# A hybrid encoder block on one core: branch A's order written out for four engines, gate traffic on ScalarE

## The chip, the cores and the metric

The kernel runs on one core of one Trainium2 chip. The metric is device time in microseconds. Five engines work side by side, each through its own stream of instructions in the order in which the program was built: TensorE (PE) multiplies matrices, VectorE (DVE) and POOL (GpSimd) work element by element, ScalarE (ACT) evaluates functions and copies, SyncE (SP) issues transfers. An instruction that waits holds up everything behind it in its stream. Transfers between SBUF (on the chip) and DRAM are carried out by 16 DMA engines after an engine has issued them; here "a store" goes to DRAM and "a load" comes from it.

## The reference

One layer of a block of 1024 positions, width 1024, with 16 meta positions ahead of them (1040 rows in all). All inputs and outputs are float32.

```
h = concat(meta, x)
proj = rms_norm(h) @ w_in            # qa, ka, va | qb, kb, vb | gate a, gate b
y_a  = differential_attention(...)   # 4 heads: softmax(q1 k1) - lam * softmax(q2 k2), times v,
                                     # bias -slope*|distance|, then rms_norm
y_b  = windowed_gqa(...)             # 8 heads, window 128, sinks
h = h + (sigmoid(ga) * (y_a @ w_ba) + sigmoid(gb) * (y_b @ w_bb)) @ w_o
h = h + (silu(f @ w_gate) * (f @ w_up)) @ w_down      # f = rms_norm(h), 2816 columns
out = rms_norm(h)[16:]
```

## The kernel before, in words

Products of float32 matrices are made of parts: an operand is split into a high part (ACT copies it to a rounded type) and a low part (POOL or DVE subtracts the high part from the operand), and three products are added: high*high, high*low, low*high. `split` at lines 117 and 118 makes both parts. Large products also use sums of blocks, so that seven products p = 1 to 7 of half the size stand for eight; the products of the two gates are done in this way, and their results are put together in DRAM: the results of p = 2, 3, 4 and 5 are copied out of PSUM by ACT (line 759) and stored (line 760); those of p = 1, 6 and 7 are added by DVE (line 756) to a kept value, which is loaded first (line 636) and stored again at line 760. A p = 3 step goes on in the PSUM bank of its p = 5 after that result was copied; p = 6, 7 and 4 go on in the bank of p = 1 in the same way. There are two such banks. Gate weights are loaded at line 624 (`gr`) and split into `gop`.

The stage that the change is about is branch A, the differential attention: 4 heads of 8 tiles of 128 queries. Per tile, map 1 and then map 0 each have three score products (line 814, 392 + 392 + 256 keys); DVE adds the distance bias and takes the minimum (line 817, accumulators `amn`), ACT takes the exponential with its sum (line 824, sums `adn`), DVE the reciprocal (line 826); POOL scales map 1 by the reciprocal and lambda (line 828), DVE joins the maps (line 837) and copies 32 columns (line 838). The joined weights of the tile before are then transposed on PE in three groups (line 849), ACT copies each out of PSUM as high part (line 852), DVE makes the low part (line 853). Every second tile the values are multiplied (line 862), every fourth one is normed (lines 869 to 885). Queries and keys of a head (`aq`, `ak`; lines 664 to 677) are loaded for map 1 and map 0 apart, as soon as the buffers are free in the last tile of the head before.

Gate products fill PE between the steps of a tile. What stands at each step is written in a string, `SLOTS = "sgsgsngsgsstntnt"`: s one score product, g one gate step (a quarter of a gate result: three products), t one group of transposes, n one part of values or norms. At the start of head 1, 2 and 3 ten gate steps come one behind the other (`G_HEAD = 10`) while the head's queries and keys arrive.

PE's order is written by hand ("manual schedule"): instructions go into PE's stream in the order of the code. For the other engines the framework's scheduler chose the order in branch A, but for the very first tile, where ACT and DVE were by hand too. At the start of the FFN (lines 1253 to 1400), DVE's order was by hand for the first twelve steps and ACT's was not. There the blocks of the normed rows are transposed, summed in pairs (`kept`, `ts`, `b`, lines 1268 to 1274) and split (line 1321, low parts 1325), and the weights are split at lines 117 and 118.

Transfers signal their end through eight semaphores, called DMAHW0 to DMAHW7 in the listings below, which all transfers of the program take in turn. A transfer whose turn has a semaphore in use waits for the transfer that uses it. Before, SP issued all of them.

## Time and profile before

| | us |
|---|---|
| median of 3 runs (lowest to highest) | 1441.89 (1441.3 to 1443.64) |
| profiled execution | 1441.88 |
| its span (first to last instruction) | 1440.0 |
| PE busy in it | 1420.1 |
| stage: norm, projections, branch B | 0 to 325 |
| stage: branch A with the gates | 325 to 615 |
| stage: sums of branches, output product | 615 to 812 |
| stage: FFN, gate and up | 812 to 1255 |
| stage: FFN, down, and final norm | 1255 to 1440 |

The ends of the stages are read from the timeline and rounded. PE is granted its full clock nearly throughout (0.998 as a mean).

How to read the rows: a row of the timeline is start, duration, engine and line, operation, what it writes and reads, shape, count; in brackets the idle time of the engine ahead of it, and what ended it. "SPq" is SP's issuing of transfers. A row of windows gives, for a stretch, its length, the busy time and number of instructions of PE, PE's weight loads, DVE, ACT and POOL, PE's granted clock, the busy share of the DMA engines and GB/s. A row of waits gives who waited, for what, the total, the number of times and the longest.

### The profile page before, as it was taken

The page shows a single profiled execution, that of the slowest core. Times are in us where ns is not written, and L with a number is a line of the kernel's source. Part 1 is how long each engine was busy: PE and PEld are TensorE (multiplying, and loading weights), DVE is VectorE, ACT ScalarE, POOL GpSimd, SP SyncE. Part 2 cuts the span into 40 slices and gives each one's busy share as a digit, 9 for nine tenths or more (in the row PEclk, how much of TensorE's full clock was granted, in tenths as well). Part 3 has the DMA queues.
Part 4 walks back from the last instruction along what each step waited for, and adds up shares of the span by engine and source line. Part 5 has one row for each costly group of instructions (what it writes and reads, how often), then busy time and mean ns, then how long its engine had stood idle before and what let it go on. Part 6 is the DMA issues. An engine that isn't in the chain of part 4 may idle for free.

```text
span 1440.0 us, 21175 instructions
## 1 busy us (share of the span) xinstructions
PE 1420.1 (99%) x7279; PEld 1219.3 (85%) x7279; DVE 899.8 (62%) x1624; ACT 680.1 (47%) x1294; POOL 643.6 (45%) x605
## 2 busy tenths in 40 slices
PE   8999999999999999999999999999999999999997
PEld 6988989988888989888888888888888888888886
DVE  7468536637787978624614886555555554787567
ACT  6366535545565656544413743333333333444444
POOL 5599127744433333334622665554454442000444
PEclk9999999999999999999999999999999999999999
DMA  8367668986657464576612535333323333964443
GB/s 246 87 211 235 194 160 275 282 284 221 181 178 257 145 224 141 175 251 207 210 49 88 162 93 176 99 106 105 110 97 101 104 103 102 340 201 142 124 129 139
DMA packets 188891, 242.41 MB, mean 168 GB/s; under 512 B 18208, under 2 KB 115936, under 8 KB 188784
## 3 DMA queue, kind: packets, MB, share of 16 engines
q1 hardware_dynamic: 188784, 241.07, 53.0%
q8 instruction: 57, 0.93, 0.3%
q14 instruction: 50, 0.41, 0.1%
HBM read 157.45 MB, written 77.00 MB: 163 GB/s over the span
## 4 chain that ended last, share of the span: by engine, by line
PE 86%; issue 3%; DMA 3%; POOL 3%; DVE 2%; ACT 2%; SPq 0%; POOLq 0%; ACTq 0%; DVEq 0%
PE pg L1347 28%; PE pd L1462 9%; PE pg L751 7%; PE ppa L796 6%; PE po L1105 6%; PE aps L814 4%; PE pp_ka L214 3%; PE pp_va L214 3%; PE pp_qa L214 3%; PE pp_qb L214 3%; PE apy L862 3%; POOL oa L118 3%; PE apt L849 2%; PE bpt L356 2%; PE bpy L362 2%
## 5 line engine op out<-in xcount | busy, mean ns | idle before, releaser
L118 POOL TENSOR_TENSOR wop<-wf,wop 128x512 fp32r<-128x512 f32 x128 | 172.0, 1348 | 165.5 <-ACT wop L117 153.1
L1347 PE MATMUL pg<-t,wop 128*128 128x512 f32 x1056 | 242.6, 389 | 0.0
L1347 PEld LDWEIGHTS pg<-t,wop 128*128 128x128 f32 x1056 | 198.3, 188 | 41.1
L1462 PE MATMUL pd<-ob,oa 128*128 128x512 f32 x924 | 210.0, 390 | 0.4 <-POOL oa L118 0.4
L1462 PEld LDWEIGHTS pd<-ob,oa 128*128 128x128 f32 x924 | 173.4, 188 | 36.9 <-POOL oa L118 0.8
L1347 PE MATMUL pg<-b,wop 128*128 128x512 f32 x792 | 183.5, 390 | 1.4 <-DVE kept L1272 1.4
L1347 PEld LDWEIGHTS pg<-b,wop 128*128 128x128 f32 x792 | 148.5, 188 | 32.3 <-issue 1.6
L751 PE MATMUL pg<-hT_hi,gop 128*128 128x512 f32 x384 | 142.4, 395 | 0.0
L117 ACT ACTIVATE wop<-wf 128x512 fp32r<-128x512 f32 x128 | 80.3, 632 | 86.9 <-PE pg L1347 47.7
L118 POOL TENSOR_TENSOR oa<-ra,oa 128x512 fp32r<-128x512 f32 x33 | 44.0, 1335 | 170.2 <-ACT oa L117 168.8
L118 POOL TENSOR_TENSOR gop<-gr,gop 128x512 fp32r<-128x512 f32 x47 | 65.5, 1395 | 102.8 <-ACT gop L117 101.7
L117 ACT ACTIVATE oa<-ra 128x512 fp32r<-128x512 f32 x77 | 48.7, 632 | 107.1 <-PE pd L1462 45.8
L824 ACT ACTIVATE as<-as,amn 128x1040 f32<-128x1040 f32 x64 | 74.5, 1164 | 48.6 <-DVE amn L817 37.7
L814 PE MATMUL aps<-ak,aq 128*128 128x392 f32 (+1 forms) x384 | 89.5, 328 | 2.7 <-DVE amn L817 2.1
L1163 DVE TENSOR_TENSOR s<-wf,wf 128x512 f32<-128x512 f32 x22 | 27.3, 1242 | 101.4 <-DMA wf<-in_w_ff_gate_dram 53.2
L1105 PE MATMUL po<-woh,mT 128*128 128x512 f32 x384 | 88.0, 390 | 0.0
L1105 PEld LDWEIGHTS po<-woh,mT 128*128 128x128 f32 x384 | 71.9, 188 | 14.8
L814 PEld LDWEIGHTS aps<-ak,aq 128*128 128x128 f32 x384 | 69.3, 188 | 16.2 <-DVE amn L817 3.3
L751 PEld LDWEIGHTS pg<-hT_hi,gop 128*128 128x128 f32 x384 | 72.3, 188 | 11.2 <-DVE gk L756 0.2
L343 POOL TENSOR_SCALAR bs<-bs,bdn 128x432 f32<-128x432 f32 (+1 forms) x64 | 41.4, 665 | 87.2 <-DVE bdn L341 74.5
L751 PE MATMUL pg<-hT_lo,gop 128*128 128x512 f32 x192 | 75.9, 395 | 0.0
L828 POOL TENSOR_SCALAR as<-as,adn,neglam 128x1040 f32<-128x1040 f32 x32 | 38.9, 1214 | 62.0 <-DVE adn L826 42.6
(292 smaller groups left out, 3101.7 us busy)
## 6 DMA issues: line engine op xcount, KB each, us to landing
ra<-aop SPq DMA_DIRECT2D x77, 256.0 KB, 2.6
wf<-in_w_ff_gate_dram SPq DMA_DIRECT2D x24, 512.0 KB, 3.8
wf<-in_w_ff_up_dram SPq DMA_DIRECT2D x24, 512.0 KB, 3.8
aop<-as SPq DMA_DIRECT2D x44, 256.0 KB, 2.1
w_c<-in_w_in_dram SPq DMA_DIRECT2D x17, 512.0 KB, 6.1
aop<-c SPq DMA_DIRECT2D x33, 256.0 KB, 2.0
ts_d<-to SPq DMA_DIRECT2D x16, 512.0 KB, 3.7
gw<-in_w_in_dram SPq DMA_DIRECT2D x32, 256.0 KB, 4.3
```

Source lines behind the costliest of these rows:

```text
L117: nc.scalar.activation(hi, src, AF.Copy)
L118: lo_eng.tensor_tensor(lo, src, f32(hi), ALU.subtract)
L214: nc.tensor.matmul(ps[:, :n], a[:, c, :], b[:, c, at:at + n], start=(c == 0 and i == 0), stop=(c == DC - 1 and i == 2))
L343: nc.gpsimd.tensor_scalar(st[:, r, :W], st[:, r, :W], dn[:, r:r + 1], 1.0, ALU.mult, ALU.mult)
L751: nc.tensor.matmul(ps, op[:, a, c], quad(b, *act)[:, c], start=(p in (2, 5, 1) and c == 0 and i == 0), stop=(p in (2, 3, 4) and c == 3 and ...
L796: nc.tensor.matmul(ps, w[:, a, j, :], src(j, b, tk), start=(j == 0 and n == 0), stop=(j == 3 and n == 2))
L814: nc.tensor.matmul(ps[:, :n], qs[m][:, t * P:(t + 1) * P], ks[m][:, vv, k0:k0 + n], start=(vv == 0), stop=(vv == 1))
L824: nc.scalar.activation(s[m][:, 0:L], s[m][:, 0:L], AF.Exp, bias=low, scale=-1.0, accum_out=dn[:, m:m + 1])
L862: nc.tensor.matmul(py[:, cols], v[:kp, a, k, :], at_[:kp, k, b, :], start=(k == 0 and j == 0), stop=(k == 8))
L1105: nc.tensor.matmul(ps, mT[:, c, a, t * P:(t + 1) * P], wos[q, c][:, b], start=(c == 0 and n == 0), stop=(c == DC - 1 and n == 2))
L1347: nc.tensor.matmul(ps, op[:, x, c, :], b[:, y, c, :], start=(p in (1, 2, 5) and c == 0 and n == 0), stop=(p in (4, 2, 3) and c == 3 and n ...
L1462: nc.tensor.matmul(ps[u], oa[:, a, u * P:(u + 1) * P], ob[:, b, :], start=(p in (1, 2, 5) and j == 0 and k == 0), stop=(p in (2, 3, 4) and ...
```

## The change

1. In all of branch A the order of ACT, DVE, POOL and SP is written by hand too.
2. In a tile, the reciprocal and the scale of map 1 come at the fifth score product, the exponential of map 0 after the first group of transposes (`EXP_AT = 1`), the join after the first score product of the next tile. Of the three low parts of a tile's transposes, the first is made at once, the second and third (and the copy of 32 columns) are put into a list `behind` and made after the next tile's first and second score product.
3. A gate result is not taken out of PSUM at once: it is put into `owed`, and taken out (`settle`) after the third and after the sixth score product of a tile, at the second quarter of the next gate, or in a burst after each step.
4. Stores of gate results and loads of gate weights are issued by ACT. Loads of kept values are issued by SP, at the second quarter of a gate (`ask_kept`). There is one more buffer each for gate results and kept values during most of branch A, taken from a pool where `yg` goes from two buffers to one.
5. Splits of gate weights (`held_back`, `let_go`) are let go at two fixed places of each tile, or just ahead of the step that needs them.
6. The load of head h+1's queries and keys stands after the third (map 1) and sixth (map 0) score product of the last tile of head h; that of its values at its third tile.
7. The table of the silu function is loaded by an activation on one column ahead of the FFN.
8. At the FFN's start ACT's order is written by hand too, and the high parts are asked for in another sequence (`HIGHS`).

PE's stream is the same in both kernels. In the listings a row is line, operation, written<-read, shape; the last digit of a name is the block of a gate or the tile. Line numbers of the changed kernel are those of its own file: 625 loads gate weights, 769 copies and 778 stores gate results, 869 is the exponential, 902 the high part of transposed weights, 118 the split's high part.

ACT at the last tile of head 0 and the first of head 1, before, with what each row waits for:

```order
L824 ACTIVATE as_1_3181,adn_7_4490<-as_1_3181,amn_7_4489 128x1040 [waits DVE_49]
L759 COPY gate_stage<-pg_3_4345 128x512 [waits DMAHW3_49,PE_49,Activation_49]
L117 ACTIVATE gop_5_4606<-gr_5_4516 128x512 [waits DMAHW5_49]
L759 COPY gate_stage<-pg_4_4609 128x512 [waits DMAHW6_49,PE_49,Activation_49]
L117 ACTIVATE gop_6_4627<-gr_6_4604 128x512 [waits DMAHW0_49]
L117 ACTIVATE gop_7_4656<-gr_7_4625 128x512 [waits DMAHW2_49,PE_49,Pool_49]
L759 COPY gate_stage<-pg_5_4630 128x512 [waits DMAHW0_49,Activation_49]
L824 ACTIVATE as_1_0_4649,adn_0_4648<-as_1_0_4649,amn_0_4647 128x1040 [waits DVE_49,Pool_49]
```

The same place in the changed kernel:

```order
L869 ACTIVATE as_1_3181,adn_7_4484<-as_1_3181,amn_7_4483 128x1040 [waits DVE_49]
L902 ACTIVATE at_6_4400<-apt_6_1_4565 128x4x128 [waits PE_49]
L902 ACTIVATE at_6_4400<-apt_6_2_4581 128x128 [waits PE_49]
L625 DMA gr_6_4590<-ws_d_101 128x512 [waits DMAHW0_49]
L769 COPY gate_stage_3_4596<-pg_3_4339 128x512 [waits DMAHW2_49,PE_49]
L778 DMA g_d_81<-gate_stage_3_4596 128x512 [waits DMAHW2_49,Activation_49]
L625 DMA gr_7_4608<-ws_d_102 128x512 [waits DMAHW3_49,Pool_49]
L769 COPY gate_stage_4_4614<-pg_4_4592 128x512 [waits DMAHW4_49,PE_49]
L778 DMA g_d_84<-gate_stage_4_4614 128x512 [waits DMAHW4_49,Activation_49]
L625 DMA gr_6_4637<-ws_d_101 128x512 [waits DMAHW5_49,Pool_49]
L769 COPY gate_stage_5_4651<-pg_5_4610 128x512 [waits DMAHW6_49,PE_49]
L869 ACTIVATE as_1_0_4629,adn_0_4628<-as_1_0_4629,amn_0_4627 128x1040 [waits DVE_49]
```

Between the copies stand five transfers that were SP's, and the splits of gate weights have moved behind. The semaphores DMAHW2 to DMAHW5 that these transfers wait for are those of head 1's `aq` and `ak` loads for map 0.

ACT at the start of head 2 in the changed kernel:

```order
L625 DMA gr_1_5402<-in_w_in_dram 128x4x128 [waits DMAHW3_49,Pool_49]
L778 DMA g_d_75<-gk_0_5226 128x512 [waits DMAHW6_49,DVE_49]
L625 DMA gr_2_5418<-in_w_in_dram 128x4x128 [waits DMAHW7_49,Pool_49]
L778 DMA g_d_77<-gk_1_5308 128x512 [waits DMAHW4_49,DMAHW0_49,DVE_49]
L869 ACTIVATE as_2_0_5431,adn_0_5430<-as_2_0_5431,amn_0_5429 128x1040 [waits DVE_49]
L778 DMA g_d_76<-gk_0_5394 128x512 [waits DMAHW5_49,DMAHW2_49,DVE_49]
L625 DMA gr_3_5467<-in_w_in_dram 128x4x128 [waits DMAHW3_49,Pool_49]
L118 ACTIVATE gop_1_5469<-gr_1_5293 128x512
```

The last row is the split of gate weight 7_1 (`gr7_1`); ahead of it stand the first tile's exponential, three stores and three loads, all of which were on SP before except for the exponential.

ACT at the start of the FFN, before:

```order
L1321 ACTIVATE t_8775<-kept_8619 128x4x128
L1372 COPY p_1_0_8858<-pg_0_1_8845 128x512
L117 ACTIVATE wop_1_1_8789<-wf_1_8787 128x512
L117 ACTIVATE wop_1_2_8792<-wf_1_8787 128x512
L1321 ACTIVATE t_8772<-ts_8874 128x4x128
L117 ACTIVATE wop_2_1_8842<-wf_2_8840 128x512
L117 ACTIVATE wop_2_2_8861<-wf_2_8840 128x512
L1270 COPY kept_8636<-ptn_f_1_8869 128x512
L1271 ACTIVATE b_8046<-ptn_f_1_8869 128x4x128
```

And in the changed kernel:

```order
L1470 COPY p_1_0_8831<-pg_0_1_8818 128x512
L1368 COPY kept_8638<-ptn_f_1_8839 128x512
L1369 ACTIVATE b_8048<-ptn_f_1_8839 128x4x128
L1417 ACTIVATE t_8775<-ts_8844 128x4x128
L118 ACTIVATE wop_1_1_8855<-wf_1_8853 128x512
L118 ACTIVATE wop_1_2_8858<-wf_1_8853 128x512
L118 ACTIVATE wop_1_1_8863<-wf_1_8861 128x512
L118 ACTIVATE wop_1_2_8866<-wf_1_8861 128x512
```

The copies `kept` and `b` of the sixth block stood behind four weight parts and a high part after the copy of `p`; now they follow it at once, and the weight parts come after them.

The diff, cut to its core:

```diff
-        nc.sync.dma_start(raw, ws_d[k][:, (5, 6, 7, 3).index(p)] if p in (5, 6, 7, 3) else
+        (nc.sync if held_back is None else nc.scalar).dma_start(raw, ws_d[k][:, (5, 6, 7, 3).index(p)] if p in (5, 6, 7, 3) else
                           g_weights(k, *{2: (1, 0), 1: (0, 0), 4: (1, P)}[p], P))
...
         if p in (1, 6, 7):
-            kept = g_kept[p, k] = gpool.tile([P, 512], F32, tag="gk", name=f"gk{p}_{k}", bufs=GK_BUFS)
-            nc.sync.dma_start(kept, g_place(p, k))
+            kept_to_do.append((p, k))
+    def ask_kept():
+        while kept_to_do and len(g_kept) < GK_BUFS + (1 if more_rooms else 0):
+            load_kept()
...
+    def gate_result(p, k, ps):
+        if p in (1, 6, 7):
+            while (p, k) not in g_kept:
+                load_kept()
+            st = g_kept.pop((p, k))
+            nc.vector.tensor_tensor(st, ps, st, ALU.add)
+        else:
+            st = room("g", G_BUFS, f"gate_stage{p}_{k}")
+            nc.scalar.copy(st, ps)
+        to_store.append((p, k, st))
...
+    def store_gates():
+        while to_store:
+            p, k, st = to_store.pop(0)
+            nc.scalar.dma_start(g_place(p, k), st)
...
     def gate_steps():
         for n, (p, k) in enumerate(order_g):
             g_ahead(n + 1)
+            while (p, k) not in g_ready:
+                let_go(1)
...
+                if c == 1 or burst[0]:
+                    settle()
+                if c == 1:
+                    ask_kept()
                 if c == 3:
-                    if p in (1, 6, 7):
-                        st = g_kept.pop((p, k))
-                        nc.vector.tensor_tensor(st, ps, st, ALU.add)
-                    else:
-                        st = gpool.tile([P, 512], F32, tag="g", name="gate_stage", bufs=G_BUFS)
-                        nc.scalar.copy(st, ps)
-                    nc.sync.dma_start(g_place(p, k), st)
+                    owed.append((p, k, ps))
...
+            if b:
+                behind.append(low)
+            else:
+                low()
...
+    order_av = tc.manual_schedule(engines={mybir.EngineType.Activation, mybir.EngineType.DVE, mybir.EngineType.Pool, mybir.EngineType.SP})
+    order_av.__enter__()
...
+            if what == "s" and n < AH * NT:
+                next(scoring)
+                scored += 1
+                if scored == 1 and n:
+                    join_a(tiles[n - 1][2])
+                    catch_up(1)
+                if scored == 2:
+                    catch_up(9)
+                if scored == 3:
+                    exp_a(s, 1)
+                    settle()
+                    if t == NT - 1 and h < AH - 1:
+                        ask_kept()
+                        ahead = load_a1(h + 1)
+                    if n == 0:
+                        let_go(1)
+                if scored == 5:
+                    scale_a(t, s)
+                    if n:
+                        let_go(1)
+                if scored == 6:
+                    settle(False)
...
+                if scored == 6 and t == NT - 1 and h < AH - 1:
+                    ahead = load_a0(h + 1, *ahead)
+            elif what == "t" and n:
+                next(turning)
+                turned += 1
+                if turned == EXP_AT and n < AH * NT:
+                    exp_a(s, 0)
+                    store_gates()
+                if turned == 3:
+                    let_go(1)
...
+    table = small.tile([P, 1], F32, tag="ss", name="table")
+    nc.scalar.activation(table, gt[:, 0:1], AF.Silu)
...
+    HIGHS = {3: ((5, 0),), 4: ((5, 1),), 5: ((5, 2, 3), (4, 0)), 6: ((4, 1, 2),), 7: ((7, 0, 1),), 8: ((7, 2, 3), (4, 3))}
     for n in range(nf):
-        if n not in range(5, 8):
+        if n == 0:
+            order_av = tc.manual_schedule(engines={mybir.EngineType.Activation, mybir.EngineType.DVE})
+            order_av.__enter__()
+        if n > 7:
             prepare()
...
         if n in AFTER:
             turn_f(AFTER[n])
             if n == 0:
-                split_t(0)
-            split_t(AFTER[n] - 4)
+                high_t(6, 0)
+            high_t(6, AFTER[n] - 4)
+            if n:
+                prepare(used[0] + 4)
         product_f(*steps[n][1])
         used[0] -= 1
+        for p, *us in HIGHS.get(n, ()):
+            high_t(p, *us)
```

More of the change, by code (lines that the diff above doesn't have):

```diff
@@ L37 @@
 N_WAIT = 3
+EXP_AT = 1
 PP2 = 2
@@ L869, in normed_a @@
         nc.scalar.activation(ysq, py, AF.Square)
[L870 removed]
+        yg = apool2.tile([P, 512], F32, tag="yg", name=f"yg_{nm}", bufs=1)
         nc.scalar.activation(yg, py, AF.Copy, scale=gsub)
+        yield
         yield
```

144 lines of the change are left out of this document (85 added, 59 removed).

## The prediction, made before the changed kernel was run

> **What bounds the kernel now.** The page's list of busy engines comes first, then the busy time of three stages, then the waits of TensorE (PE) inside branch A.
>
> ```profile
> PE 1420.1 (99%) x7279; PEld 1219.3 (85%) x7279; DVE 899.8 (62%) x1624; ACT 680.1 (47%) x1294; POOL 643.6 (45%) x605
> ```
>
> PE is busy 1420.1 us of a span of 1440.0 us, so the whole program holds 19.9 us in which PE has nothing to do. No reordering of the other engines can give more than that. The stages, as time, busy time and instructions of each engine:
>
> ```profile
> 325.00:615.00 290.00, 285.56 (x1736) 256.57 (x1735) 231.81 (x655) 170.71 (x322) 116.71 (x93) 1.00 0.58 190
> 615.00:812.00 197.00, 197.00 (x899) 163.68 (x898) 85.39 (x107) 82.80 (x145) 77.93 (x67) 1.00 0.50 160
> 812.00:1255.00 443.00, 441.56 (x1952) 365.55 (x1951) 263.94 (x304) 172.62 (x296) 206.41 (x151) 1.00 0.39 126
> ```
>
> Branch A runs from 325 to 615 us. PE idles there for 290.00 - 285.56 = 4.4 us; the next stage has no idle time, and the FFN's first two products have 443.00 - 441.56 = 1.4 us. These are all the stages that the change touches, so at most 5.9 us of idle time stand in its reach. Who makes PE wait in branch A (us in all, times, longest):
>
> ```profile
> PE aps L814 <- DVE amn L817: 2.1, 5, 0.7
> PE apt L849 <- DVE as L837: 1.1, 2, 1.0
> PE aps L814 <- DMA ak<-ka_d: 0.5, 1, 0.5
> PE apf L883 <- DVE amn L817: 0.3, 1, 0.3
> PE apt L849 <- DVE amn L817: 0.2, 1, 0.2
> ```
>
> Ten waits, 4.2 us: nine for VectorE (DVE) and one for a load of keys. Each costs PE a little more than its idle time, because its pipeline runs empty. At the wait for the keys two score products start 0.90 us apart with 0.55 us idle (393.90 and 394.80, below); unhindered, a pair takes 0.52 us and one 0.34, so starts are 0.18 us apart. The wait cost 0.72 us, 0.17 more than its idle time, and I put that on each wait, an estimate from this one place. So branch A's waits are worth at most 4.2 + 10 x 0.17 = 5.9 us.
>
> **The FFN's start.** ScalarE (ACT), VectorE and PE there:
>
> ```profile
> 811.86 1.15 ACT L117 ACTIVATE wop<-wf 128x512 fp32r<-128x512 f32 x2
> 812.90 0.58 ACT L1270 COPY kept<-ptn_f 128x512 f32<-128x512 f32 x1
> 813.52 0.69 DVE L1272 TENSOR_TENSOR kept<-kept,ptn_f 128x512 f32<-128x512 f32 x1 [3.48 <-ACT kept L1270]
> 814.36 1.86 PE L1347 MATMUL pg<-b,wop 128*128 128x512 f32 x7 [1.44 <-DVE kept L1272]
> ```
>
> ACT makes weight parts until 812.90 before it copies the sixth block's sum; DVE has stood idle for 3.48 us for that copy, and PE then stands for 1.44 us. With ACT in hand order the copy stands ahead of the four weight parts, so it comes two to three us sooner and this wait goes: at best -1.6 us (1.44 and 0.17). What is late next is the weight part itself, which moves behind the copy: two pairs of 1.15 us in front of a POOL subtraction of about 1.35 us (the page's L118 row, quoted under the second head) end at 813 to 814, against PE's 813 or so. At worst 0.6 us of it stays, and the gain is 1.0. I take **-1.3**. The silu table's load leaves this place too; ACT is behind nobody there at 816, and it is worth nothing.
>
> **Scaling ahead of the low parts, gate results at two places.** The rows of DVE and ACT keep their number and kind; only their order changes. Of the ten waits, four stand at heads: the keys 0.55, `amn` at 399.15 and at 467.41, 0.45 each, and the one of 0.2; they are taken up below. The six others hold 4.2 - 1.6 = 2.6 us idle and 6 x 0.17 us more, 3.7 us in all. The longest is the 1.0 of `as L837`: a join that comes late. The new order puts join and scale ahead of the second and third low part, and a copy of 0.58 us no longer comes between an exponential and the reduction that needs its bank. I expect most of this to go, not all, as DVE remains at 231.81 / 290 = 80% busy: **-2.4**, between 0 and -3.7. The 97 transfers that ACT now issues take its time; what that costs is the second rival.
>
> **Transfers on ACT at the heads' beginnings.** This is where the change adds a wait. All transfers take their completion signals in turn from eight; a ninth is not issued before the first of the eight has landed. The rows of SP's queue show it: start, length of the issue, line.
>
> ```profile
> 377.74 0.32 SPq L671 DMA_DIRECT2D aq<-qa_d  x1
> 378.17 0.36 SPq L760 DMA_DIRECT2D g_d<-gate_stage  x1
> 378.59 0.42 SPq L664 DMA_DIRECT2D ak<-ka_d  x1
> 379.06 1.21 SPq L666 DMA_DIRECT2D ak<-ka_d  x2
> 380.36 0.53 SPq L677 DMA_DIRECT2D aq<-qa_d  x1
> 380.94 0.43 SPq L664 DMA_DIRECT2D ak<-ka_d  x1
> 381.42 0.46 SPq L666 DMA_DIRECT2D ak<-ka_d  x1
> 382.56 0.46 SPq L666 DMA_DIRECT2D ak<-ka_d  x1
> 384.42 0.32 SPq L624 DMA_DIRECT2D gr<-ws_d  x1
> 385.75 0.32 SPq L760 DMA_DIRECT2D g_d<-gate_stage  x1
> 387.25 0.38 SPq L624 DMA_DIRECT2D gr<-in_w_in_dram  x1
> 389.78 0.32 SPq L760 DMA_DIRECT2D g_d<-gate_stage  x1
> 392.27 0.38 SPq L624 DMA_DIRECT2D gr<-in_w_in_dram  x1
> ```
>
> Queries and keys of head 1 are asked for at 377.74 to 382.56. After that SP stands at each small transfer until one of them has landed: 384.42, 385.75, 387.25, 389.78, 392.27. Those instants are the landings. Before, only SP stood. Now the small transfers (gate weights in, gate results out) are in ACT's stream, so ACT stands in SP's place, and behind it stand its copies of gate results, transposed weights and exponentials. PE's rows there:
>
> ```profile
> 389.81 0.52 PE L814 MATMUL aps<-ak,aq 128*128 128x392 f32 x2
> 390.18 0.40 PE L751 MATMUL pg<-hT_hi,gop 128*128 128x512 f32 x1
> 393.90 0.34 PE L814 MATMUL aps<-ak,aq 128*128 128x392 f32 x1
> 394.80 0.42 PE L814 MATMUL aps<-ak,aq 128*128 128x392 f32 x1 [0.55 <-DMA ak<-ka_d]
> 399.15 0.62 PE L814 MATMUL aps<-ak,aq 128*128 128x392 f32 x2 [0.45 <-DVE amn L817]
> ```
>
> In the changed order of ACT the copy of gate result 5_4 stands behind the store of 3_3 (it waits for `aq`, 389.78) and a weight load (it waits for `ak`, 392.27). The copy can then start at about 392.3 and takes 0.58 us: 392.9. The gate step that begins at 390.18 adds into that bank and needs the copy. PE stands for 392.9 - 390.2 = 2.7 us. An earlier copy, of 3_3, waits for the landing that SP saw at 385.75 and just meets PE's need. Against the 2.7 us stands the wait for keys, 0.72 us with its refill, which PE then reaches late enough to find no more, but the exponential of the next tile, behind two more such transfers, follows no sooner than now. I take **+2.5**. From below: 0, if the banks or the order give ACT a way round that I misread. From above: +6, if the landings themselves move (third rival).
>
> At head 2 (gates of p = 1, 6, 7, whose results DVE adds):
>
> ```profile
> 451.74 0.54 SPq L666 DMA_DIRECT2D ak<-ka_d  x1
> 461.30 0.32 SPq L636 DMA_DIRECT2D gk<-g_d  x1
> 464.05 2.24 SPq L636 DMA_DIRECT2D gk<-g_d  x2
> 462.03 1.17 ACT L824 ACTIVATE as<-as,amn 128x1040 f32<-128x1040 f32 x1
> 462.76 0.39 PE L751 MATMUL pg<-hT_hi,gop 128*128 128x512 f32 x1
> 467.41 0.62 PE L814 MATMUL aps<-ak,aq 128*128 128x392 f32 x2 [0.45 <-DVE amn L817]
> L118 POOL TENSOR_TENSOR gop<-gr,gop 128x512 fp32r<-128x512 f32 x47 | 65.5, 1395 | 102.8 <-ACT gop L117 101.7
> ```
>
> The last of head 2's keys, asked for at 451.74, lands before 464.05: that transfer waits for its turn of the semaphores. Since PE runs on without a wait at 462.76, I put the landing at about 462.4. On ACT now come, one behind the other: a store that waits for those keys (462.4), the exponential (1.36 us with its accumulator, 463.8), a store that waits for a kept value that SP reads only after the keys, a load, and then the split of gate weight 7_1, 0.63 us, to be followed by POOL's 1.4 us. So the low part of 7_1 is there at 463.8 + 0.63 + 1.4 = 465.8 if the store doesn't hold ACT, and at 467.4 if the kept value lands at 465.4. PE uses that low part at 462.76. It stands for 3.0 to 4.6 us, less the wait at 467.41 and a smaller one before it (0.6 us idle, 1.0 us with refill), which the delay covers. I take **+3.4**, within 0 and +5.4. At head 3 no copy stands in the blocked stretch and the kept values are asked for in time; nothing.
>
> **The sum**, on the profiled execution's 1441.88 us (span 1440.0 and 1.9 around it; the median of the runs is 1441.89): 1441.9 - 1.3 - 2.4 + 2.5 + 3.4 = 1444.1 us.
>
> **The rivals.**
>
> *The blocks are hidden.* For it speaks how ACT stood still before at little cost:
>
> ```profile
> ACT gate_stage L759 <- DMA g_d<-gate_stage: 8.1, 2, 5.2
> ```
>
> It waited 8.1 us in two waits for gate stores, 5.2 of them just here at head 1, and PE lost only 0.72 us to the keys and 1.0 at and before 399.15. If banks and weights run far enough ahead, heads 1 and 2 cost nothing and give back some of their old waits: 1441.9 - 1.6 - 3.7 = 1436.6, and 1434 with all waits gone. Against it: the named copy and the named split each have a direct user on PE.
>
> *ACT paces the tiles.* Ends slower. Place: from the last reduction of a tile's first map to the exponential of its second. ACT has there an exponential 1.36, a copy 0.58, a store and a load of 0.32 each by SP's rows, a split 0.63, a transposed part 0.60: 3.8 us, against half a tile, 290 / 32 / 2 = 4.5 us. It decides from 0.7 us of lateness on. One of the two issues, 0.32 us, in half of the 24 tiles with a copy adds 3.8 us: 1447.9. Against it: ACT is busy 170.71 of 290 us.
>
> *The landings move.* Head 1's 3.1 MB take from 377.74 to the end of PE's wait at 394.80, 17 us, so 256 KB are worth 1.4 us. Before, the small transfers were behind the keys in SP's queue. If ACT's are served beside them, four of them put the last key 5.6 us later, at 400.3, where PE would be at 396.6: 3.7 us more at head 1, and three at head 2 some 4 us: 1452. The Trainium skill, "DMA: Bandwidth & Descriptors", section "Queues, rings and completion order", says that SP and ACT own a row of rings each on the same engines, which take turns between rows packet by packet; by that rule the sharing happens. The trace of before has no transfer from ACT and shows neither.
>
> *Only the FFN's part works* and branch A's waits come back elsewhere in equal measure: 1440.6.
>
> **How the numbers follow.** Forecast 0.45, blocks hidden 0.25, ACT paces 0.15, landings move 0.08, FFN alone 0.07. A measurement of this kernel tells from no change about 0.2%, 2.9 us. The forecast's own range is 1440.5 to 1448; it gives 0.02 faster, 0.25 same, 0.18 slower. Hidden gives 0.23 faster and 0.02 same; ACT's pace 0.14 slower and 0.01 same; moved landings 0.08 slower; the FFN alone 0.01 and 0.06. In all: faster 0.26, same 0.34, slower 0.40. The range goes from 1436 (most of the hidden case) to 1450 (ACT's pace).
>
> **What would show it.** PE's waits should no longer name `kept` at the FFN's start; `amn` and `as` should fall from 3.7 us to under 2. New waits of gate products for ACT's copy near 390 and for ACT's or POOL's `gop` near 463 should show, 2 to 5 us each, with ACT's DMA queue waiting for `ak`. If those two are missing, the first rival holds; if small waits for `amn` stand in tile after tile, the second; if the wait for `ak` itself is several us long, the third.

## The result, and the profile after

The changed kernel takes 1462.97 us (median of 4 runs, 1461.81 to 1464.34) against 1441.6 us for the kernel before (1440.0 to 1443.64): a ratio of 1.0148 with a 95% interval from 1.0136 to 1.0161. It is 21 us slower; 1444.1 within 1436 to 1450 was predicted. The profiled execution took 1462.75 us and spans 1461.0 us, 21.0 more than before.

From PE's waits in the whole changed kernel, those that bear on the change (who waited for what; us in all, times, longest):

```profile
PE aps L856 <- DVE at L904: 5.8, 9, 1.2
PE pg L797 <- ACT gop L118: 3.7, 1, 3.7
PE pg L1445 <- DVE p L1459: 3.0, 1, 3.0
...
PE pg L797 <- POOL gop L119: 2.1, 2, 1.6
...
PE aps L856 <- DVE amn L859: 1.5, 4, 0.5
...
PE aps L856 <- DMA g_d<-gate_stage: 0.8, 1, 0.8
...
PE pg L797 <- ACT gate_stage L769: 0.5, 1, 0.5
```

The wait for `kept` at the FFN's start is gone, and so is the one for keys at head 1. Waits for `amn` remain, 1.5 us instead of 2.1. The others are new: score products that wait for low parts of transposed weights (line 904), gate products that wait for a split, and one FFN product that waits 3.0 us for a result. The 0.8 us put down to a store stand at 348.75, at the place of a tile where the next tile but one waits 0.85 us for line 904; I count them with that row.

PE executes the same 7279 products in the same order in all kernels here, so the n-th product of one trace can be set against the n-th of another. The difference of their starts, less its value at the first score product of tile 2 (338 us; there it is -0.9 to 2.8 us in kernels that are the same up to branch A, which is what one execution tells no better), gives where the time goes. Where two kernels have the same branch A, a stretch of it differs by up to 1.4 us between their traces, so a difference of this size in one stretch of one trace says little:

```
stretch of the kernel before (us)           changed kernel later by (us)
338 to 385   tiles of head 0                 5.9
385 to 462   head 1 and its tiles            0.6
462 to 468   first tile of head 2            5.9
468 to 519   other tiles of head 2           2.1
519 to 587   head 3 to the last tiles        2.8
587 to 812   sums, output product            0.0
812 to 816   FFN, sixth block's copy        -1.7
816 to 847   FFN, next eleven steps          4.9
847 to end                                   0.6
whole, with -0.2 before 338                 21.0   (parts are rounded)
```

### A tile

The same half tile in both kernels, at the change from tile 6 to tile 7 of head 0. The `...` in a listing stands for rows left out. ACT before:

```profile
373.42 1.16 ACT L824 ACTIVATE as<-as,amn 128x1040 f32<-128x1040 f32 x1 [1.26 <-DVE amn L817]
...
374.58 0.58 ACT L852 ACTIVATE at<-apt 128x512 fp32r<-128x512 f32 x1
...
376.21 0.75 ACT L852 ACTIVATE at<-apt 128x512 fp32r<-128x512 f32 x2
377.56 0.59 ACT L759 COPY gate_stage<-pg 128x512 f32<-128x512 f32 x1 [0.60 <-ACT at L852]
378.04 0.63 ACT L117 ACTIVATE gop<-gr 128x512 fp32r<-128x512 f32 x1
```

The scheduler had put the first transposed group (line 852) right behind the exponential of map 1, and the gate's copy and split last. The changed kernel, ACT with its transfers (ACTq), then DVE and PE:

```profile
377.80 1.16 ACT L869 ACTIVATE as<-as,amn 128x1040 f32<-128x1040 f32 x1 [1.80 <-DVE amn L859]
...
378.96 0.56 ACT L769 COPY gate_stage<-pg 128x512 f32<-128x512 f32 x1
379.55 0.33 ACTq L778 DMA_DIRECT2D g_d<-gate_stage  x1
379.91 0.46 ACTq L625 DMA_DIRECT2D gr<-ws_d  x1
380.41 0.63 ACT L118 ACTIVATE gop<-gr 128x512 fp32r<-128x512 f32 x1 [0.89 <-ACT gate_stage L769]
380.95 0.58 ACT L902 ACTIVATE at<-apt 128x512 fp32r<-128x512 f32 x1
```

```profile
381.56 0.69 DVE L904 TENSOR_TENSOR at<-apt,at 128x512 fp32r<-128x512 f32 x1 [1.86 <-ACT at L902]
...
382.24 0.62 DVE L859 CUSTOM_DVE_ANT_0 as<-aps,dist,far_a 128x392 f32<-128x392 f32 x1
```

```profile
382.31 0.63 PE L856 MATMUL aps<-ak,aq 128*128 128x392 f32 x2 [1.23 <-DVE at L904]
```

Between the exponential and the transposed group now stand the copy, its store, a load and the split: 380.95 - 378.96 = 2.0 us. Of these 0.89 us are idle time of ACT: the store has to wait until the copy is finished, the load is issued behind the store, and only then does the split start. DVE's next row is the low part of that group, and DVE stands idle for 1.86 us until the group is there. Transposes and score products take their PSUM banks from the same five (lines 854 and 896). The low part is the last reader of the group's bank, and PE waits 1.23 us for it: the score product starts at 382.31, where the low part ends (381.56 and 0.69). The next tile's first reduction comes behind it and is late too.

### Head 2

ACT and PE in the changed kernel, and PE's granted clock (the last number but two) in two stretches of 2 us:

```profile
467.09 0.34 ACTq L778 DMA_DIRECT2D g_d<-gk  x1
467.97 0.37 ACTq L625 DMA_DIRECT2D gr<-in_w_in_dram  x1
468.61 0.38 ACTq L778 DMA_DIRECT2D g_d<-gk  x1
469.76 1.16 ACT L869 ACTIVATE as<-as,amn 128x1040 f32<-128x1040 f32 x1 [9.69 <-DVE amn L859]
...
470.92 0.34 ACTq L778 DMA_DIRECT2D g_d<-gk  x1
471.36 0.39 ACTq L625 DMA_DIRECT2D gr<-in_w_in_dram  x1
471.80 1.15 ACT L118 ACTIVATE gop<-gr 128x512 fp32r<-128x512 f32 x2 [0.79 <-DMA gr<-in_w_in_dram]
```

```profile
472.48 0.80 PE L797 MATMUL pg<-hT_hi,gop 128*128 128x512 f32 x1 [3.69 <-ACT gop L118]
```

```profile
474.40:476.40 2.00, 2.00 (x7) 1.69 (x6) 0.63 (x2) 0.00 (x0) 0.00 (x0) 0.50 0.04 12
478.40:480.40 2.00, 2.00 (x17) 1.96 (x17) 0.94 (x4) 1.87 (x4) 2.00 (x2) 1.00 0.00 0
```

The split of gate weight 7_1 starts at 471.80, behind three transfers, the exponential and two more transfers, and PE stands for 3.69 us. The exponential started when DVE's last reduction was done (`amn`); the three transfers ahead of it had been issued by then. After the wait PE runs at half its clock for some 6 us (472.4 to 478.4), which costs some 3 us more: set product against product, PE's lag grows by 3.8 us over the wait and by another 2.9 us behind it. The products from 474.4 to 476.4 come at less than half the rate of those from 478.4 on (7 against 17 in 2 us).

### Head 1

SP's first request for head 1 and ACT behind it in the changed kernel, then PE:

```profile
383.89 0.33 SPq L689 DMA_DIRECT2D aq<-qa_d  x1
```

```profile
388.02 0.33 ACTq L778 DMA_DIRECT2D g_d<-gate_stage  x1
...
393.67 0.33 ACTq L778 DMA_DIRECT2D g_d<-gate_stage  x1
395.65 0.33 ACTq L625 DMA_DIRECT2D gr<-ws_d  x1
396.07 0.59 ACT L769 COPY gate_stage<-pg 128x512 f32<-128x512 f32 x1 [3.31 <-PE aps L856]
```

```profile
396.71 0.50 PE L797 MATMUL pg<-hT_hi,gop 128*128 128x512 f32 x1 [0.49 <-ACT gate_stage L769]
```

ACT stands at a store and a load until keys and queries have landed, as predicted, but the landings come 9.8 and 11.8 us after the first request (393.67 and 395.65 less 383.89). Before they came 12.0 and 14.5 us after it (389.78 and 392.27 less 377.74). PE waits 0.49 us for the copy. These figures scatter: in the run below with the FFN as before, whose branch A is the changed kernel's, they are 10.5 and 13.0 us and PE waits 1.6 us; in the run that changes only the FFN of the kernel before they are 11.4 and 13.4 us.

### The FFN

POOL, DVE and PE in the changed kernel, and behind them two rows of DVE before:

```profile
828.34 6.12 POOL L119 TENSOR_TENSOR wop<-wf,wop 128x512 fp32r<-128x512 f32 x4 [7.40 <-ACT wop L118]
835.74 6.57 POOL L119 TENSOR_TENSOR wop<-wf,wop 128x512 fp32r<-128x512 f32 x4 [1.28 <-ACT wop L118]
```

```profile
839.55 1.61 DVE L1262 TENSOR_TENSOR wf<-wf 128x512 f32<-128x512 f32 x1
...
855.53 1.18 DVE L1421 TENSOR_TENSOR t<-ts,t 128x512 fp32r<-128x512 f32 x1
856.63 5.14 DVE L1421 TENSOR_TENSOR t<-kept,t 128x512 fp32r<-128x512 f32 x3
...
862.30 0.68 DVE L1459 TENSOR_TENSOR p<-pg,p 128x512 f32<-128x512 f32 x1
```

```profile
863.03 5.30 PE L1445 MATMUL pg<-t,wop 128*128 128x512 f32 x15 [3.05 <-DVE p L1459]
```

```profile
830.53 0.69 DVE L1164 TENSOR_TENSOR wf<-wf 128x512 f32<-128x512 f32 x1
...
837.08 1.18 DVE L1325 TENSOR_TENSOR t<-ts,t 128x512 fp32r<-128x512 f32 x1
```

The copy of the sixth block comes in time, as predicted. But the weight parts that stood ahead of it are late: POOL is idle for 7.40 us and starts them at 828.34, and its work of that time, and later the low parts of p = 4, now run beside DVE's. The same row of DVE (839.55, before 830.53) takes 1.61 us while POOL subtracts (835.74 to 842.31), where it took 0.69 us before. DVE's row at 855.53 stands at 837.08 in the kernel before, 18.4 us earlier, while PE is 15.4 us behind by the table: DVE is already 3.0 us late there. Three more subtractions of 1.7 us each follow, then the result `p`. PE stands for 3.05 us, and runs at half clock for 3.4 us again.

### The profile page after: what moved, and what is told of

Its sections match the earlier page's. It is cut to its first block, busy times and chain, and to the rows that moved or that the text cites. A ratio compares the mean times of both kernels' runs of the same rounds, so it can differ in the third digit from the quotient of the medians.

```text
span 1461.0 us, 21123 instructions
## 1 busy us (share of the span) xinstructions
PE 1427.6 (98%) x7279; PEld 1220.6 (84%) x7279; DVE 901.7 (62%) x1624; ACT 677.5 (46%) x1295; POOL 647.5 (44%) x605
## 3 DMA queue, kind: packets, MB, share of 16 engines
q10 hardware_dynamic: 19968, 25.17, 5.3%
## 5 line engine op out<-in xcount | busy, mean ns | idle before, releaser
L856 PEld LDWEIGHTS aps<-ak,aq 128*128 128x128 f32 x384 | 69.0, 190 | 25.9 <-DVE at L904 10.1
```

Of the source, the lines that this page charges most:

```text
L856: nc.tensor.matmul(ps[:, :n], qs[m][:, t * P:(t + 1) * P], ks[m][:, vv, k0:k0 + n], start=(vv == 0), stop=(vv == 1))
```

## The experiments

Three theories stood against each other at first. One: ACT's stream is what is late (rows that stand ahead of the transposed group and of the split). Two: DVE's order, scaling ahead of low parts, is what is late. Three, for the FFN: its wait is its own, or handed on from branch A. The stretches below are those of the table above, in us against the kernel before. The code cuts show the core of each edit; `...` marks what is left out.

### Transfers back on SP

```diff
-        (nc.sync if held_back is None else nc.scalar).dma_start(raw, ...
+        nc.sync.dma_start(raw, ...
-            nc.scalar.dma_start(g_place(p, k), st)
+            nc.sync.dma_start(g_place(p, k), st)
```

> The changed kernel with its gate stores and gate weight loads issued by SP again, still in the hand order; nothing else differs. Theory (ScalarE's stream is what is late: in a tile its store and load issues stand ahead of the split and the first transposed group, 0.9 us, for which VectorE waits and behind VectorE the next score product; at head 2 its stores and loads stand behind the keys' landings and the split of gate weight 7_1 behind them): the lag of TensorE behind the kernel before at the end of head 0 falls from 6.1 us to under 3, the 3.7 us wait at head 2 for the split goes, in all 9 to 13 us less than the changed kernel's 1463: 1450 to 1454. Rival (the order of VectorE, scaling ahead of low parts, is what is late): no more than 3 us less, 1460 or more.

1460.9 us, ratio to the kernel before 1.0137 (1.0121 to 1.0152). Head 0's tiles: 0.5 instead of 5.9. Head 2's first tile 4.2 instead of 5.9, its others 0.5 instead of 2.1. But head 1 rises from 0.6 to 3.5 and head 3 from 2.8 to 6.8. PE's waits, and SP's between 515 and 552 us:

```profile
PE aps L856 <- DMA ak<-ka_d: 6.3, 5, 1.6
```

```profile
SPq L778 <- DVE gk L766: 11.4, 2, 6.0
```

So the issues on ACT are what makes the tiles of head 0 late, as theory one has it. The total hardly fell, because in SP's hand order a store of a gate result holds up the keys of the next head until DVE has added that result: SP stands 11.4 us in two such waits, and PE 6.3 us for keys, 3.0 of them at head 1 and 3.3 at head 3. At head 2 ACT issues nothing any more and 4.2 us stay (PE still waits 2.8 us for the split): there it is not the transfers in the main.

### The FFN's start as before

```diff
-    HIGHS = {3: ((5, 0),), 4: ((5, 1),), 5: ((5, 2, 3), (4, 0)), ...}
-            order_av = tc.manual_schedule(engines={Activation, DVE})
+            order_dve = tc.manual_schedule(engines={DVE})
...
+            split_t(AFTER[n] - 4)
```

> The changed kernel with the FFN's start as it was before (ScalarE's order left to the scheduler, high parts in the old sequence). Theory (the new start gains 1.7 us at the sixth block's copy and loses 4.5 us some 33 us later, where VectorE makes three low parts beside POOL ahead of a result that TensorE waits for): the 3.0 us wait for that result goes and the 1.4 us wait at the start comes back; 2.5 to 3.5 us less than 1463. Rival (the wait 33 us later is only handed on from branch A, by loads that come at other times): it stays, and the time is 1.5 us more.

1460.92 us, 1.0142 (1.0127 to 1.0157): 2 us less than the changed kernel. Both effects go together: -1.7 becomes 0.0, 4.9 becomes 0.0, with branch A as late as ever. The FFN's loss is its own, and theory three falls in its second form.

### Low parts at once

```diff
-            if b:
-                behind.append(low)
-            else:
-                low()
+            low()
...
-        behind[1:1] = [lambda: nc.vector.tensor_copy(...)]
+        nc.vector.tensor_copy(...)
```

> The changed kernel with the second and third low part made at once and the 32-column copy right behind the join, as before. Theory (ScalarE is late, not VectorE's order): not better, 0 to 4 us more than 1463, since the low parts now stand ahead of the join. Rival (VectorE's order is what is late): 4 to 8 us less, and the waits of score products for the low part of transposed weights go.

1494.41 us, 1.037 (1.0354 to 1.0386), 31 us more than the changed kernel. Head 0's tiles cost 15.1, the others of head 2 10.9. PE's largest wait:

```profile
PE apt L899 <- DVE amn L859: 16.4, 17, 1.7
```

DVE now stands for two or three transposed groups of ACT, one behind the other, before it joins and reduces, so that transposes wait for it as well. Putting off the low parts, and with them the copy of 32 columns, is worth 31 us in this order. I had expected 0 to 4 us. Theory two falls with this, and with the run further down that keeps DVE's order as the changed kernel has it and brings the tiles of head 0 to 0.5.

### Two rows of ACT moved

```diff
                     exp_a(s, 1)
-                    settle()
+                    settle(False)
...
                     scale_a(t, s)
-                    if n:
-                        let_go(1)
...
+                if turned == 1:
+                    let_go(1)
```

> The changed kernel with two rows moved on ScalarE: the store of a gate result goes behind the exponential of map 0 instead of right behind its copy, and the split of gate weights that was let go at the fifth score product goes behind the first transposed group. All transfers stay on ScalarE. Theory: the first transposed group comes 0.35 plus 0.63 us sooner, the lag over head 0 (6.1 us) falls under 2 us, that over the tiles of head 2 (2.9 us) under 1; head 2's own 6 us stay; 6 to 9 us less than 1463. Rival (VectorE's order): within 2 us of 1463.

1467.21 us, 1.0184 (1.0167 to 1.0201), 4 us more. Head 0's tiles: 1.9 instead of 5.9, as theory one has it. But from head 3 on it is 10.2 instead of 2.8:

```profile
PE pg L797 <- ACT gop L118: 5.5, 4, 2.8
PE pg L797 <- POOL gop L119: 4.2, 4, 1.5
```

With the split behind the transposed group, gate weights come late: between 530 and 560 us PE waits 1.5 us for ACT's part and 1.5 us for POOL's, and the clock is halved for 6.8 us behind that. Why at these places was not looked into. The store, too, did not go where I had meant it to: the next gate step's own `settle` issues it, so it only changed places with the load.

### The store behind the load

Only the first of the two edits (`settle(False)` at the third score product).

> The changed kernel with one row moved per tile: the store of the gate result that is copied after the third score product stands behind the exponential of map 0, no longer right behind its copy; the split stays where the changed kernel has it. Theory: ScalarE stands still for the copy's end and the store's issue (0.3 to 0.5 us a tile, by rows of the changed kernel) before the split and the transposed group; without it the lag over head 0 falls from 6.1 to between 2 and 4 us, while the late splits that cost 5 us in heads 3 and 4 of the kernel with both rows moved do not come, so in all 3 to 5 us less than 1463: 1458 to 1460. Rival (the gain there came from the split alone): head 0's lag stays at 6 us, time within 1.5 us of 1463.

1457.65 us, 1.0113 (1.0097 to 1.013): 5 us less than the changed kernel. Head 0's tiles 3.8, head 2's others 1.1. The order of ACT shows that this is copy, load, store, split: the load's issue now falls into the running exponential, and ACT's idle time before the split is 0.40 us instead of 0.89. The split stays where it was, so the late weights of the run before do not come.

### The split of p = 7 in the burst

```diff
-        for i, (what, far) in enumerate(((g_load, GR_BUFS - 1), (g_split, GO_BUFS - 1))):
...
+        while held_back and burst[0] and held_back[0] <= n + 1 and order_g[held_back[0]][0] == 7:
+            let_go(1)
+        while g_done[0] < min(n + GR_BUFS - 1, len(order_g)):
+            g_load(g_done[0])
+            g_done[0] += 1
```

In the burst of gate steps at a head's start the split of p = 7 is let go as soon as its step is next, and the loads for later steps are asked for behind it.

> The changed kernel with the split of the gate weights of p = 7 let go inside the burst of gate steps at head 2, before the loads that wait for the keys, no longer just ahead of its step. Theory (the split's place behind the exponential costs 5 us, the transfers around it 1 to 2): the wait of gate products for the split, 3.7 us, and that for its low part go; the lag over head 2's first tile falls from 6 us to 1 to 2; 4 to 5 us less than 1463. Rival (the block by the keys' landings is what is late): another wait, for the kept values or the exponential, takes its place there, and no more than 1.5 us are gained.

1458.21 us, 1.0108 (1.0093 to 1.0124), 5 us less than the changed kernel. The first tile of head 2: -0.7 instead of 5.9. No other wait takes its place between 455 and 480 us, though ACT still stands at transfers there. Standing at the landings was harmless by itself; the split's place behind the exponential and the transfers was not.

### Three mends together

The two last edits and the FFN as before.

> The changed kernel with the store behind the exponential, the split of p = 7 inside the burst and the FFN's start as before. If the parts add up (3 to 5, 4 to 5, 3 us), 11 to 12 us less than 1463: 1451; what is left to 1441.6 is the second and third head's tiles and head 3's gate. If they do not add, over 1455.

1448.89 us, 1.0046 (1.0033 to 1.006), 14 us less than the changed kernel: the parts (5, 5 and 2 us) add, with 2 us more, in stretches 3.5 in head 0, 0.1, -1.1, 1.4, 1.9, FFN 0.0. I had expected 1451.

### The store truly behind the exponential

```diff
                 if c == 1 or burst[0]:
-                    settle()
+                    settle(burst[0])
```

> The kernel with three mends, with the store of a gate result now really behind the exponential of map 0 (in the kernel before it had only changed places with the weight load, since the next gate step stored it). Theory (ScalarE stands 0.40 us a tile between a copy's end and the split, waiting to issue the store): the split follows the copy without idle time, the lag over head 0 falls from 4.1 to about 2 us and that of head 2's tiles by half: 2 to 3 us less than 1448.9, 1446 to 1447. Rival (the store's place no longer matters): within 1 us of 1448.9.

1444.35 us, 1.0018 (1.0008 to 1.0029), 4.5 us less than the three mends. Head 0's tiles: 0.5; other tiles of head 2: 0.1. ACT at the place shown above:

```profile
373.61 1.16 ACT L876 ACTIVATE as<-as,amn 128x1040 f32<-128x1040 f32 x1 [1.80 <-DVE amn L866]
373.74 0.33 ACTq L625 DMA_DIRECT2D gr<-ws_d  x1
...
374.77 0.56 ACT L776 COPY gate_stage<-pg 128x512 f32<-128x512 f32 x1
375.24 0.63 ACT L118 ACTIVATE gop<-gr 128x512 fp32r<-128x512 f32 x1
375.56 0.33 ACTq L785 DMA_DIRECT2D g_d<-gate_stage  x1
375.77 0.58 ACT L909 ACTIVATE at<-apt 128x512 fp32r<-128x512 f32 x1
376.25 1.16 ACT L876 ACTIVATE as<-as,amn 128x1040 f32<-128x1040 f32 x1
```

ACT has no idle time left between exponential and transposed group. Both transfers are still its own, 0.33 us each; load and store are now issued while an ACTIVATE runs and cost nothing. In the code the store stands behind the exponential of 376.25; the trace has its issue at 375.56, so an issue can run ahead of rows whose turn on the engine has not come. So it is not the issue that costs but the place of a store right behind the row that makes its data.

### The split behind the group, in heads 0 and 1

```diff
                     scale_a(t, s)
-                    if n:
+                    if n >= 2 * NT:
                         let_go(1)
...
+                if turned == 1 and n < 2 * NT:
+                    let_go(1)
```

> The kernel of e12 with the split of gate weights behind the first transposed group in heads 0 and 1 only (where it was in e6 and cost nothing). Theory: another 0.6 us a tile off the path in head 0; its lag falls to 0 to 1 us, in all 1 to 2 us less than e12: 1444 to 1446. Rival (VectorE alone limits the tile now): same as e12.

1445.66 us, 1.0032 (1.0021 to 1.0043). Not better: head 0 2.2 and head 1 2.0 instead of 0.5 and -0.1. The split's 0.6 us are no longer on the path; its lateness is: from 325 to 460 us PE waits 2.9 us for parts of gate weights (2.1 for POOL's, 0.8 for ACT's) instead of 0.6, and behind one of these waits, 1.49 us at 341.82, the clock is halved for 3.4 us.

### The FFN, two other ways

ACT by hand in the old sequence, copies ahead of the next weight parts, on the kernel before, and on the kernel of the last run:

```diff
-        if n not in range(5, 8):
+        if n not in (2, 4, 5, 6, 7):
             prepare()
...
             turn_f(AFTER[n])
+            if n:
+                prepare()
```

> The kernel before with only the FFN's start changed, in a smaller way: ScalarE by hand for the first twelve steps, in the old sequence of high parts, with the copies of a block's sum ahead of the next weight parts. Theory (the late copy behind weight parts costs 1.6 us; the 4.5 us later come from the new sequence of high parts): the 1.4 us wait goes, no new wait 33 us later, 1440.0, 1 to 2 us less than before. Rival (the hand order of ScalarE itself brings the later wait): 3 us more than before.

> The kernel of e13 with the FFN's start of e11 (ScalarE by hand, copies ahead of the next weight parts). e11 gained 1.0 us at the copy and lost 1.1 us later against the kernel before: within 1 us of e13.

On the kernel before: 1442.65 us, 1.0004 (0.9995 to 1.0013), no difference that can be told, where I had expected 1 to 2 us less; the trace has -1.0 at the copy and 1.2 some 30 us later. On the other: 1445.49 us, 1.0023 (1.0013 to 1.0032), with -1.0 and 1.1. What a copy gains by going first, the weight parts behind it lose.

### POOL's parts of p = 4 into its idle time

```diff
-    HIGHS = {3: ((5, 0),), 4: ((5, 1),), 5: ((5, 2, 3), (4, 0)), 6: ((4, 1, 2),), 7: ((7, 0, 1),), 8: ((7, 2, 3), (4, 3))}
+    HIGHS = {1: ((4, 0, 1),), 3: ((5, 0), (4, 2)), 4: ((5, 1),), 5: ((5, 2, 3),), 6: ((4, 3),), 7: ((7, 0, 1),), 8: ((7, 2, 3),)}
```

> Branch A as in e12, the FFN's start as in the changed kernel, but the four high parts of p = 4, whose low parts POOL makes, asked for at the second, fourth and seventh step instead of the sixth to ninth, so that two of POOL's 1.7 us subtractions run in its idle 7.4 us. Theory (POOL and VectorE slow each other: VectorE's subtractions of two SBUF operands take 1.6 to 1.8 us beside POOL and 0.7 without, and that is why a result is 3 us late): the 3.0 us wait falls under 1.5 us, the 1.7 us gain at the sixth block's copy stays, and the time is 1441 to 1444, at or under e12's 1444.35. Rival (the place of VectorE's last low parts alone): the wait stays at 3 us or more, 1446 to 1448.

1443.15 us, 1.0007 (0.9998 to 1.0016), the fastest version of the change: not told apart from the kernel before. The FFN keeps -1.7 and loses 0.3 instead of 4.9; the 3.0 us wait is gone. DVE there:

```profile
838.58 1.18 DVE L1428 TENSOR_TENSOR t<-ts,t 128x512 fp32r<-128x512 f32 x1
839.69 4.08 DVE L1428 TENSOR_TENSOR t<-kept,t 128x512 fp32r<-128x512 f32 x3
```

The row of three low parts takes 4.08 us instead of 5.14, and the row ahead of it is 1.0 us late against PE instead of 3.0 (838.58 less 837.08, with PE 0.5 us behind). DVE's low parts kept their places. That POOL's subtractions standing beside DVE's were the cause is shown as far as this: moving them, with ACT's four high parts that feed them, takes the wait away. Which share is slower subtractions and which a shorter queue on POOL and ACT was not tried apart.

## Why the prediction was wrong

The direction that the sum gave, slower, was right, but it was put at 2 us, and the range ended at 1450. By the table, the tiles of heads 0 and 2 cost 8.0 us where -2.4 stood, head 2's first tile 5.9 instead of 3.4, the FFN 3.2 instead of -1.3, head 3 2.8 instead of nothing, and head 1 0.6 instead of 2.5. Step by step:

**What bounds it, and how much is to be gained.** Right as far as it went: the waits named were the ones in reach, and even the best version gains nothing measurable. What I left out was the other side: 99% busy PE says how little can be won, not how much can be lost.

**The FFN's start, -1.3.** Its gain measured -1.7. The step failed in what it said is late next: I looked one product ahead, at the weight part needed at 813 us, and found cover for it. The weight parts were late in POOL's stream, which worked beside DVE 15 to 35 us on, and a result 33 us behind the copy was late by 3.0 us. That cost 4.9, half clock included. With POOL's parts moved the step comes out as priced (-1.7 and 0.3).

**Scaling ahead of the low parts, -2.4.** This is the step that failed most. Of the six old waits the join's at 519 did go (the stretch from 518 to 519 gains 1.1 us in the changed kernel), but the tiles cost 5.9 us in head 0 and 2.1 in head 2. I had read DVE's share, 80%, and the number of its rows, and not the order of ACT's rows ahead of the group for which DVE waits. The place I did name, as the rival "ACT paces the tiles": exponential, copy, store, load, split, transposed part. It had 0.15 and a price of 3.8 us. The price failed twice. I set the 3.8 us of these rows against half a mean tile, 4.5 us. That mean spreads the gate bursts of the heads over all tiles; inside a head the tiles of the kernel before follow one another about 7.5 us apart on the mean, half of which is 3.75, so the 0.7 us of slack were not there. And I counted an issue as 0.32 us, where a store behind its own copy holds ACT for the copy's end as well: 0.89 us idle for a store and a load. Its sign was named wrong too: the small waits that stand in the tiles are for the low part `at` (line 904, 5.8 us in nine waits), not for `amn`. With the store behind the exponential, both are free and the tiles are at 0.5.

**Head 1, +2.5.** The mechanism is there and the size was wrong: ACT stands in SP's place, and PE waits for the copy behind it, but 0.49 us instead of 2.7, because queries and keys land 2.3 to 2.8 us sooner after their request than before. In the other trace with the same branch A they land later and the wait is 1.6 us. The whole head and its tiles cost 0.6 us in the one trace and 1.9 in the other.

**Head 2, +3.4.** The place was right, and the split of 7_1 behind the exponential as its cause. PE's wait was 3.69 us, within the predicted 3.0 to 4.6, but in part by luck: the exponential started behind DVE's last reduction, some 1 us later than I had put it behind the keys' landing (469.76 less the 6.3 us that PE is behind there is about 463.5, against 462.4), and PE waited for ACT's high part alone and not for POOL's 1.4 us as well. The size was off by what follows such a wait: I counted 0.17 us for a wait's end, and PE ran at half clock for some 6 us. The stretch cost 5.9. That the blocked transfers were not the main cause is shown by the run that moved the split ahead (-0.7) and by the run with all transfers on SP (4.2).

**Head 3, nothing.** There is a wait of 1.6 us for POOL's part of a gate weight near 553; the stretch to the last tiles costs 2.8, and 1.8 to 1.9 in the mended kernels. I had not looked at POOL there, and no run took it apart; it stays open.

**The rivals.** "The landings move" came out the other way round at head 1: the landings moved, but to be earlier. The Trainium skill, "DMA: Bandwidth & Descriptors", section "Queues, rings and completion order", says that the DMA engines take turns between SP's row and ACT's, which lets one expect that requests of ACT hold up the keys. The trace agrees that there is a second queue (19968 packets, none before) and that it is served beside the first: ACT's store of 388.02 took 8.3 us to land, the two key loads issued just ahead of it, from 387.07 on, 10.1 us. The keys came sooner all the same. Why is open. ACT's requests were not later: the first after the keys stands 4.1 us behind SP's first request (388.02 less 383.89), where SP's stood 6.7 us behind it (384.42 less 377.74); but before, a gate store stood in the midst of the key requests as well (378.17), and a part of the difference is scatter.

## What to carry to other kernels

Here an engine that issued the transfer of data that it had just made stood until that row had ended and the transfer was issued, 0.40 us idle for a store, and everything behind it stood too; with two or three independent rows between the result and its store the same transfer was free. When an order is written by hand, follow for each engine the row that another engine waits for, and add up all that now stands ahead of it; shares of busy time and numbers of rows do not show it. Where a stall is removed by moving work back, look for where that work lands, tens of microseconds on, and which engine it then runs beside.

## What was not expected of the hardware

PE's clock. After waits of 1.44 us (the FFN before) and 1.57 us (553 us, after) the granted clock stays at 1.00. After 3.69 us it is 0.50 for 6.0 us, and after the 3.05 us of the FFN 0.64 as a mean of the next 4 us. In the run with transfers on SP, waits of 2.8 and 0.6 us, 0.8 us apart, were followed by 0.50 and 0.66 in the next two stretches of 2 us. But in the run with the split behind the group in heads 0 and 1, one wait of 1.49 us (341.82) was enough: the length of a wait alone does not tell. In the clock's own records every stretch at 0.50 outside the last microseconds of a kernel lasts 3.41 us or twice that (471.57 to 478.40 and 864.11 to 867.52 in the changed kernel, 342.89 to 346.30 in that run). The Trainium skill, "TensorE: Matmul & The Clock Gate", section "Part 1: The HAM clock gate (the "warmup" mystery)", says that about 3.4 us without work halve the clock, and about as long with work restores it. The traces agree on the return, in steps of 3.41 us; on the wait they differ, since 3.05 us and even 1.49 us were enough. At half the clock 3.41 us do the work of 1.7 us, so each such stretch costs up to 1.7 us on top of the wait, an estimate from these records: a stall of 3 us on PE can cost nearly twice itself.

A transfer issued by ACT takes 0.33 to 0.46 us of ACT's queue in the rows shown, and none of its time while an ACTIVATE is running: the load issued at 373.74 lies inside the exponential from 373.61 on.
